# Attention on one core: the powers transposed 64 queries at a time, in two halves of the array

## The chip, the cores and the metric

The kernel runs on one core of a Trainium2 chip. A core has TensorE (PE in the profile; its weight loads are listed as PEld), VectorE (DVE), ScalarE (ACT), GpSimd (POOL) and SyncE (SP), each with its own queue of instructions, and 16 DMA engines. The metric is the device time of one execution in microseconds, lower is better; the median of the runs is compared.

## The reference, cut to what matters

One inference step of a two-layer network over 1024 prompt tokens and 32 sample tokens of width 1024: a recurrent layer (RG-LRU), then shared keys and values, then one layer of attention in a sliding window with 16 heads of 64 in 4 groups (g), and a sink per head. Keys come in chunks of 64: a query sees its own chunk and the two before it.

```python
s = jnp.einsum('bnqkgd,bnskd->bnkgqs', qb, kb).astype(jnp.float32) * scale
...
s = jnp.where(valid[None, :, None, None, None, :], s, -jnp.inf)
sink = sinks.astype(jnp.float32).reshape(N_KV_HEADS, GROUP)[None, None, :, :, None, None]
p = sink_softmax(s, sink)      # exp(s - m) / (sum exp(s - m) + exp(sink - m))
o = jnp.einsum('bnkgqs,bnskd->bnqkgd', p.astype(vb.dtype), vb)
```

Everything is float32. The kernel gets its accuracy from float32r matmuls by splitting each operand into a high and a low part.

## The kernel before, in words

Channels lie on partitions and tokens in columns, in three blocks of about 384 tokens. The recurrent layer and the projections of k and v come first; the attention begins at 549 us and ends at 826 us of the span; the output projection of the rest and the last norms follow.

The attention loops over the 4 groups g, and in each over nine stages j: j = 0 to 7 are 128 queries of the prompt each, for the group's 4 heads (nh = 4), j = 8 the 32 sample tokens, whose 4 heads share the 128 rows (nh = 1). A stage sees nk blocks of 128 keys: one for j = 0, two for the others. One stage has four steps:

- stage_s: S matmuls (L984), queries on the rows; VectorE takes the negated maximum (L986) and ScalarE the powers exp(s - m) with their sum (L989) into the tile P, 128 queries x nh heads x keys.
- stage_n: P is divided by the sum, two heads on ScalarE (L999), two on VectorE (L1001).
- stage_t: P has to be transposed, keys on partitions, for the next matmul. In a transpose on TensorE, P's 128 x 128 block is loaded as weights and the identity `ident` is passed through. The results of the nh heads for one block of keys go into one PSUM bank T (tag "T", two banks). `split` (L128, L129) moves each bank into ph (ScalarE, rounded to float32r) and pl (VectorE, the remainder).
- stage_o: O = V times ph and pl, summed over the blocks of keys in one bank (L1019). V holds a high and a low part in 64 columns each, so rows 64 to 127 of O are copied aside by ScalarE (L1021, `oh`) and added by VectorE (L1027) into the output tile TT, one head at a time.

Between the steps the loop in `_trunk` draws from a generator `fillers(g)`: matmuls of the gates (`gB`), of the next group's queries (`rAq`, `rBq`) or of the output projection (`obm`), all at L757. The order of each engine's queue isn't the order of this code: a scheduler that simulates the engines chooses it when the program is built. `pin` keeps an instruction in the order of the code in relation to others that are pinned. Each queue is then worked through strictly in the order that the scheduler left.

Of the kernel before, what the change touches and what calls it, by code (L numbers as in the profile page):

```python
# [10 lines left out]
F32R = mybir.dt.float32r  # L11
AF = mybir.ActivationFunctionType
ALU = mybir.AluOpType
# [4 lines left out]
P = 128  # L18
# [57 lines left out]
def _trunk(ctx, tc, nc, A):  # L76
    V, S, G = nc.vector, nc.scalar, nc.gpsimd
# [13 lines left out]
    def pin(i, on=True):  # L91
        return tc.keep_in_program_order(i) if on else i

    def bank(name, tag="mm", bufs=None):
        return psum.tile([P, 512], F32, tag=tag, name=name, bufs=bufs or nbank)
# [28 lines left out]
    def split(dst_hi, dst_lo, src, lo_eng=None, hi_dve=False, behind=False):  # L124
        if hi_dve:
            V.tensor_copy(dst_hi, src)
        else:
            pin(S.activation(dst_hi, src, AF.Copy), behind)  # L128
        (lo_eng or V).tensor_tensor(dst_lo, src, dst_hi.bitcast(F32), op=ALU.subtract)  # L129
# [131 lines left out]
    ident = cst.tile([P, P], F32, name="ident")  # L261
# [218 lines left out]
    half = {}  # L480
# [57 lines left out]
    def unit(name, dt=F32, w=384):  # L538
        return units.tile([P, 416], dt, tag="u", bufs=NU, name=name)[:, :w]
# [81 lines left out]
    for n in range(3):  # L621
        for m in LATE:
            w = NSB[n][1] - NSB[n][0]
            hl = [late.tile([P, 384], F32R, tag="t", bufs=NT, name=f"y{x}{m}_{n}")[:, :w] for x in "hl"]
# [86 lines left out]
    for n, order in enumerate(orders):  # L711
        zs, acc = {}, []
        w = NSB[n][1] - NSB[n][0]
# [25 lines left out]
    def att_tile(name, shape, dt, tag, bufs):  # L739
        return att.tile([P] + shape, dt, tag=tag, bufs=bufs, name=name)  # L740

    def kv_tile(name, shape, dt, tag, bufs=1):
        return kvp.tile([P] + shape, dt, tag=tag, bufs=bufs, name=name)
# [159 lines left out]
    QU, KU, VU, SG, TT = {}, {}, {}, {}, {}  # L903
# [56 lines left out]
    def stage_s(g, j):  # L960

        smp = j == 8
        n = 2 if smp else j // 3
        if (g, n) not in KU:
            load_kv(g, n)
        nm = f"{g}_{j}"
        nh, nk = (1 if smp else 4), (1 if j == 0 else 2)
        t0 = 3 if smp else max(j - 1, 0) - KB0[n] // P
        w = nk * P
        ks = slice(t0 * P, t0 * P + 256)  # L970
        sm = att_tile(f"sm{nm}", [3, 4], F32, "sm", 4)
        nmax, rsum, rl = (sm[:, i, :nh] for i in range(3))
        sk = slice(16 + g, 17 + g) if smp else slice(4 * g, 4 * g + 4)
        msk = smask if smp else mask[:, 256 - w:]

        pt = att_tile(f"P{nm}", [4, 258], F32, "P", 2)
        S.activation(pt[:, :nh, w:w + 1], nsnk[:, sk].unsqueeze(2), AF.Copy)
        for h0 in range(0, nh, 2):
            sb = bank(f"S{nm}_{h0}", "S", 2)
            for h in range(h0, min(h0 + 2, nh)):  # L980
                q = QS[g].rearrange("p h c -> p (h c)") if smp else QU[g, n][:, h, P * j - NSB[n][0]:P * j - NSB[n][0] + P]
                s = sb[:, (h - h0) * 256:(h - h0) * 256 + 256]
                for hl in range(2):
                    pin(nc.tensor.matmul(s, q, KU[g, n][:, hl, ks], start=hl == 0, stop=hl == 1), g == 0 and j == 0)  # L984
            for h in range(h0, min(h0 + 2, nh)):
                V.tensor_tensor_reduce(pt[:, h, :w], sb[:, (h - h0) * 256:(h - h0) * 256 + w], msk,  # L986
                                       -0.125, nsnk[:, sk][:, h:h + 1], op0=ALU.add, op1=ALU.min,
                                       accum_out=nmax[:, h:h + 1])
                S.activation(pt[:, h, :w + 1], pt[:, h, :w + 1], AF.Exp, bias=nmax[:, h:h + 1], scale=-1.0,  # L989
                             accum_out=rsum[:, h:h + 1])  # L990
        return dict(P=pt, nh=nh, nk=nk, t0=t0, n=n, nm=nm, smp=smp, w=w, rsum=rsum, rl=rl)
# [9 lines left out]
                V.tensor_scalar(pt[:, h, :w], pt[:, h, :w], rl[:, h:h + 1], None, op0=ALU.mult)  # L1001

    def stage_t(st):
        nm, w = st["nm"], st["nh"] * P
        st["p"] = []
        for kt in range(st["nk"]):
            tb = bank(f"T{nm}_{kt}", "T", 2)[:, :w]
            for h in range(st["nh"]):
                nc.tensor.transpose(tb[:, h * P:(h + 1) * P], st["P"][:, h, kt * P:(kt + 1) * P], ident)  # L1009
            hl = [att_tile(f"p{x}{nm}_{kt}", [512], F32R, "p" + x, 2)[:, :w] for x in "hl"]  # L1010
            split(*hl, tb)
            st["p"].append(hl)

    def stage_o(g, j, st):
        n, w, nk = st["n"], st["nh"] * P, st["nk"]
        ob = bank(f"O{st['nm']}", "O", 1)[:, :w]
        for kt in range(nk):
            for i, x in enumerate(st["p"][kt]):
                nc.tensor.matmul(ob, VU[g, n][:, st["t0"] + kt, :], x, start=kt + i == 0, stop=kt == nk - 1 and i == 1)  # L1019
        half = kv_tile(f"oh{st['nm']}", [512], F32, "oh")  # L1020
        S.activation(half[:64, :w], ob[64:128], AF.Copy)  # L1021
        q = w // 4
        c0 = 256 if st["smp"] else P * j - NSB[n][0]
        if (g, n) not in TT:
            TT[g, n] = [unit(f"T{g}_{n}_{i}", w=NSB[n][1] - NSB[n][0]) for i in range(2)]
        for h in range(4):
            V.tensor_tensor(TT[g, n][h // 2][64 * (h % 2):64 * (h % 2) + 64, c0:c0 + q],  # L1027
                            ob[:64, h * q:(h + 1) * q], half[:64, h * q:(h + 1) * q], op=ALU.add)

    ogl = {}  # L1030

# [87 lines left out]
    for g in range(4):  # L1119
        fil = fillers(g)  # L1120
        per = PER[g]
        todo = [0, 1, 2]
        st = {0: stage_s(g, 0)}
        stage_n(st[0], False)
        for j in range(9):
            if j < 8:
                st[j + 1] = stage_s(g, j + 1)
            if g == 0 and j == 0:
                for _ in range(2):
                    next(fil)  # L1130
            stage_t(st[j])
            if j < 8:
                stage_n(st[j + 1])
            for _ in range(per - (g == 3 and j > 6)):
                next(fil, None)
            stage_o(g, j, st.pop(j))
            while todo and j >= (2, 5, 8)[todo[0]] and (2 * g + 1, todo[0]) in SG:
                finish_og(g, todo.pop(0))
        if g == 3:
            break  # L1140
        run(fil)
        for n in todo:
            finish_og(g, n)
# [176 lines left out]
```

## Time and profile before

| | |
|---|---|
| median of 3 runs | 897.91 us (897.18 to 900.01) |
| the profiled execution | 896.39 us, of which its span is 894.6 us |
| TensorE busy | 881.0 us, 5462 matmul passes, mean clock granted 0.997 |
| weight loads busy | 863.1 us |
| VectorE, ScalarE, GpSimd busy | 702.3, 563.6, 211.5 us |

Busy shares are shares of the span. Matmuls overlap in the pipeline and their ends are modelled, so the durations of neighbouring matmuls add up to more than the time they take; the step from one start to the next tells what one costs. In rows of groups the columns are the shape (rows*columns of the array, then partitions x elements), the count after x, the busy time in us, the mean duration in ns, and the idle time of the engine ahead of them. Rows of the timeline begin with start and length in us and end with the number of instructions merged in them. Rows of a tile's table give the shortest, median and longest duration in ns, then first and last start in us. Rows of the table of stretches give the stretch and its length in us, busy time and count for PE, PEld, DVE, ACT and POOL, the granted clock, the DMA share and GB/s.

### The profile page before, as it was taken

Reading aid. Unit: us, or ns where it says so; the run is one execution under the profiler, and the core shown is the slowest. Engines: PE = TensorE matmul, PEld = TensorE weight load, DVE = VectorE, ACT = ScalarE, POOL = GpSimd, SP = SyncE. Lnnn points to the kernel's source line nnn. Section 1 sums busy time; section 2 is a strip of 40 time slices with the busy share of each in tenths; the row PEclk is TensorE's granted clock in tenths of the full one; section 3 lists DMA queues with packets and bytes.
Section 4 is the critical chain, followed back from the end, with each engine's and each line's share of the span. In section 5 each row is a group of like instructions: output and inputs, shape, how many; then the busy total and the mean of one; then the engine's idle time right before and its main releaser. Section 6 shows DMA issues by size and latency. Waiting matters only on the chain.

```text
span 894.6 us, 15865 instructions
## 1 busy us (share of the span) xinstructions
PE 881.0 (98%) x5462; PEld 863.1 (96%) x5462; DVE 702.3 (79%) x1511; ACT 563.6 (63%) x1233; POOL 211.5 (24%) x257
## 2 busy tenths in 40 slices
PE   9999999999999999999998999999999999999996
PEld 8999999999999999999997999999999999999996
DVE  5877878879897654176889847879999999898777
ACT  7848878789354325355675317756767767797652
POOL 5260212134300001124343532113023011002240
PEclk9999999999999999999999999999999999999999
DMA  9533433352544226446455568336448338444984
GB/s 335 199 107 108 118 100 120 110 147 86 182 128 126 91 55 209 136 133 202 145 171 175 190 183 231 97 101 192 115 125 228 99 120 233 118 135 123 300 259 170
DMA packets 96129, 138.76 MB, mean 155 GB/s; under 512 B 16224, under 2 KB 64128, under 8 KB 96048
## 3 DMA queue, kind: packets, MB, share of 16 engines
q1 hardware_dynamic: 86232, 124.24, 45.6%
q10 hardware_dynamic: 9640, 12.96, 4.8%
q8 instruction: 43, 0.70, 0.3%
q0 software_dynamic: 176, 0.54, 0.2%
q14 instruction: 38, 0.31, 0.1%
HBM read 99.54 MB, written 32.13 MB: 147 GB/s over the span
## 4 chain that ended last, share of the span: by engine, by line
PE 66%; DVE 4%; ACT 2%; DMA 2%; issue 1%; POOL 1%; SPq 0%; DVEq 0%; ACTq 0%; POOLq 0%
PE gB L757 10%; PE rAq L757 5%; PE rBq L757 5%; PE obm L757 5%; PE oa L168 5%; PE oa L167 5%; PE oa L169 5%; PE gb L167 4%; PE gb L168 4%; PE gb L169 4%; PE S L984 3%; PE O L1019 3%; PE T L1009 3%; PE ot L757 2%; PE rAk L757 1%
## 5 line engine op out<-in xcount | busy, mean ns | idle before, releaser
L167 PE MATMUL oa<-yh,whi_outa 128*128 128x384 f32 (+1 forms) x264 | 85.8, 326 | 0.0
L168 PE MATMUL gb<-xlo,whi_ina 128*128 128x384 f32 (+1 forms) x264 | 85.6, 324 | 0.0
L167 PE MATMUL gb<-xhi,whi_ina 128*128 128x384 f32 (+1 forms) x264 | 85.3, 323 | 0.1
L169 PE MATMUL gb<-xhi,wlo_ina 128*128 128x384 f32 (+1 forms) x264 | 85.4, 323 | 0.0
L169 PE MATMUL oa<-yh,wlo_outa 128*128 128x384 f32 (+1 forms) x264 | 85.2, 323 | 0.0
L168 PE MATMUL oa<-yl,whi_outa 128*128 128x384 f32 (+1 forms) x264 | 85.1, 323 | 0.0
L675 POOL TENSOR_TENSOR qp<-qp,qp 128x384 f32<-128x384 f32 (+2 forms) x34 | 42.2, 1242 | 178.5 <-ACT qp L673 166.4
L168 PE MATMUL br<-xlo,whi_ina 128*128 128x384 f32 (+1 forms) x240 | 77.7, 324 | 0.0
L167 PE MATMUL br<-xhi,whi_ina 128*128 128x384 f32 (+1 forms) x240 | 77.7, 324 | 0.0
L169 PE MATMUL br<-xhi,wlo_ina 128*128 128x384 f32 (+1 forms) x240 | 77.5, 323 | 0.0
L129 DVE TENSOR_TENSOR wlo_outa<-raw_outa,whi_outa 128x512 fp32r<-128x512 f32 (+1 forms) x60 | 43.0, 731 | 43.1 <-ACT whi_outa L128 42.9
L989 ACT ACTIVATE P<-P,sm 128x257 f32<-128x257 f32 (+1 forms) x132 | 64.3, 489 | 13.1 <-DVE sm L986 12.8
L757 PE MATMUL gB<-xl,whi_g 128*128 128x384 f32 (+1 forms) x192 | 63.1, 329 | 0.0
L757 PE MATMUL gB<-xh,whi_g 128*128 128x384 f32 (+1 forms) x192 | 63.1, 329 | 0.0
L128 ACT ACTIVATE whi_outa<-raw_outa 128x512 fp32r<-128x512 f32 (+1 forms) x60 | 35.5, 594 | 43.4 <-PE oa L168 23.9
L757 PE MATMUL gB<-xh,wlo_g 128*128 128x384 f32 (+1 forms) x192 | 62.8, 327 | 0.0
L986 DVE CUSTOM_DVE_ANT_0 P<-S,mask,nsnk 128x256 f32<-128x256 f32 (+1 forms) x128 | 53.1, 461 | 5.5 <-PE S L984 5.4
L257 DVE SCALAR_TENSOR_TENSOR conv<-ext,pa,conv 128x1060 f32<-128x1060 f32 (+2 forms) x51 | 46.1, 926 | 11.0 <-ACT conv L255 10.5
L167 PEld LDWEIGHTS gb<-xhi,whi_ina 128*128 128x128 f32 x264 | 49.7, 188 | 0.4 <-DVE u L565 0.4
L167 PEld LDWEIGHTS oa<-yh,whi_outa 128*128 128x128 f32 x264 | 49.6, 188 | 0.4
L168 PEld LDWEIGHTS oa<-yl,whi_outa 128*128 128x128 f32 x264 | 49.6, 188 | 0.4
L169 PEld LDWEIGHTS oa<-yh,wlo_outa 128*128 128x128 f32 x264 | 49.7, 188 | 0.0
(316 smaller groups left out, 2889.4 us busy)
## 6 DMA issues: line engine op xcount, KB each, us to landing
raw_ina<-w_in_a SPq DMA_DIRECT2D x44, 256.0 KB, 3.6
raw_outa<-w_out_a SPq DMA_DIRECT2D x40, 256.0 KB, 3.1
raw_ob<-w_out_b SPq DMA_DIRECT2D x32, 256.0 KB, 3.2
qscr<-quadq SPq DMA_DIRECT2D x8, 768.0 KB
Q<-qscr SPq DMA_DIRECT2D x32, 192.0 KB, 3.8
hscr<-u SPq DMA_DIRECT2D x11, 530.0 KB, 2.7
xr<-xr SPq DMA_DIRECT2D x8, 512.0 KB, 8.9
raw_g<-w_in_b SPq DMA_DIRECT2D x16, 256.0 KB, 5.2
```

Source lines behind the costliest of these rows:

```text
L128: pin(S.activation(dst_hi, src, AF.Copy), behind)
L129: (lo_eng or V).tensor_tensor(dst_lo, src, dst_hi.bitcast(F32), op=ALU.subtract)
L167: pin(nc.tensor.matmul(ps, wh, xh, start=i == 0, stop=False), behind and i == 0 or mid and i == n // 2)
L168: nc.tensor.matmul(ps, wh, xl, start=False, stop=False)
L169: nc.tensor.matmul(ps, wl, xh, start=False, stop=last and i == n - 1)
L257: V.scalar_tensor_tensor(c, e[:, c0 + k:c1 + k], pa[:, t, k:k + 1], c, op0=ALU.mult, op1=ALU.add)
L675: G.tensor_tensor(sums[0], sums[0], q, op=ALU.add)
L757: nc.tensor.matmul(ps, l, r, start=c == 0, stop=c == 3 * n - 1)
L984: pin(nc.tensor.matmul(s, q, KU[g, n][:, hl, ks], start=hl == 0, stop=hl == 1), g == 0 and j == 0)
L986: V.tensor_tensor_reduce(pt[:, h, :w], sb[:, (h - h0) * 256:(h - h0) * 256 + w], msk, -0.125, nsnk[:, sk][:, h:h + 1], op0=ALU.add, op1=AL ...
L989: S.activation(pt[:, h, :w + 1], pt[:, h, :w + 1], AF.Exp, bias=nmax[:, h:h + 1], scale=-1.0, accum_out=rsum[:, h:h + 1])
L1009: nc.tensor.transpose(tb[:, h * P:(h + 1) * P], st["P"][:, h, kt * P:(kt + 1) * P], ident)
```

## The change

A transpose now takes 64 queries instead of 128: half i of the queries lies on partitions 64 i to 64 i + 63, so its load uses that half of the array's rows (128 columns as before), with the matching 64 x 64 block of the identity passed through. Each half has a T bank of its own, for all heads and all blocks of keys, and the instructions alternate between the halves and are pinned. A bank is then split at once into half of ph and pl: these are now one tile each per stage, for both blocks of keys, with the columns of a block ordered by half of queries, then head, then query. stage_o's adds read that order; for j = 8 each half holds two heads and nothing is reordered.

```diff
     def stage_t(st):
-        nm, w = st["nm"], st["nh"] * P
-        st["p"] = []
-        for kt in range(st["nk"]):
-            tb = bank(f"T{nm}_{kt}", "T", 2)[:, :w]
-            for h in range(st["nh"]):
-                nc.tensor.transpose(tb[:, h * P:(h + 1) * P], st["P"][:, h, kt * P:(kt + 1) * P], ident)
-            hl = [att_tile(f"p{x}{nm}_{kt}", [512], F32R, "p" + x, 2)[:, :w] for x in "hl"]
-            split(*hl, tb)
-            st["p"].append(hl)
+        nm, nh, nk = st["nm"], st["nh"], st["nk"]
+
+        hl = [att_tile(f"p{x}{nm}", [2, 512], F32R, "p" + x, 1) for x in "hl"]
+        tb = [bank(f"T{nm}_{i}", "T", 2)[:, :nk * nh * 64] for i in range(2)]
+        for kt in range(nk):
+            for h in range(nh):
+                for i in range(2):
+                    r = slice(64 * i, 64 * i + 64)
+                    c = (kt * nh + h) * 64
+                    pin(nc.tensor.transpose(tb[i][:, c:c + 64], st["P"][r, h, kt * P:(kt + 1) * P], ident[r, r]))
+        for i in range(2):
+            split(*(x[:, :nk, i * nh * 64:(i + 1) * nh * 64] for x in hl),
+                  tb[i].rearrange("p (k c) -> p k c", k=nk))
+        st["p"] = [[x[:, kt, :nh * P] for x in hl] for kt in range(nk)]
...
         for h in range(4):
-            V.tensor_tensor(TT[g, n][h // 2][64 * (h % 2):64 * (h % 2) + 64, c0:c0 + q],
-                            ob[:64, h * q:(h + 1) * q], half[:64, h * q:(h + 1) * q], op=ALU.add)
+            dst = TT[g, n][h // 2][64 * (h % 2):64 * (h % 2) + 64, c0:c0 + q]
+            if smp:
+                a, b = (x[:64, h * q:(h + 1) * q] for x in (ob, half))
+            else:
+                a, b = (x[:64, :512].rearrange("p (i h c) -> p i h c", i=2, h=4)[:, :, h, :] for x in (ob, half))
+                dst = dst.rearrange("p (i c) -> p i c", i=2)
+            V.tensor_tensor(dst, a, b, op=ALU.add)
```

The program has 5675 matmuls instead of 5427 (248 transposes become 496), and four more splits on each of ScalarE and VectorE; no other count of working instructions differs. What the scheduler makes of it shows in TensorE's queue. In the rows, T_5_0 is stage j = 5 with the block of keys (before) or the half of queries (after) as the last index; further numbers are buffers. First, group g = 0 around the transposes of j = 5, before:

```order
L1019 MATMUL O_4_6799<-ph_4_1_6744,V_1_6468 128x512
L984 MATMUL S_6_2_6829<-K_2_6810,Q_2_6192 128x256 x2
L1019 MATMUL O_4_6799<-pl_4_1_6745,V_1_6468 128x512
L984 MATMUL S_6_2_6829<-K_2_6810,Q_2_6192 128x256 x2
L1009 MATMUL T_5_0_6838<-ident,P_5_6710 128x128 x4
L1009 MATMUL T_5_1_6847<-ident,P_5_6710 128x128 x4
L757 MATMUL rAq_1_6872<-xh_1_4834,whi_qA_0_6657 128x384
```

The same place in the changed program:

```order
L1013 MATMUL T_5_0_6871<-ident,P_5_6735 128x64
L757 MATMUL rAq_1_6909<-xl_1_4835,whi_qA_0_6682 128x384
L757 MATMUL rAq_1_6909<-xh_1_4834,wlo_qA_0_6683 128x384
L1024 MATMUL O_4_6830<-pl_4_6756,V_1_6481 128x512
L1024 MATMUL O_4_6830<-ph_4_6755,V_1_6481 128x512
L1024 MATMUL O_4_6830<-pl_4_6756,V_1_6481 128x512
L1013 MATMUL T_5_1_6872<-ident,P_5_6735 128x64
L1013 MATMUL T_5_0_6871<-ident,P_5_6735 128x64
L1013 MATMUL T_5_1_6872<-ident,P_5_6735 128x64
```

The first transpose of half 0 now stands alone, ahead of the end of the stage before; the other 15 follow behind it in one run (three of them are shown). This is so in 27 of the 36 stages, which makes 63 separate runs of transposes in all; before, there are 57.

Second, group g = 3 around the end of the transposes of j = 2, before:

```order
L1009 MATMUL T_2_0_9365<-ident,P_2_9218 128x128 x2
L1019 MATMUL O_1_9326<-pl_1_1_9253,V_0_9068 128x512
L1009 MATMUL T_2_0_9365<-ident,P_2_9218 128x128 x2
L1009 MATMUL T_2_1_9374<-ident,P_2_9218 128x128 x4
L757 MATMUL gB_1_9388<-xl_1_4911,whi_g_0_9152 128x384
L757 MATMUL gB_1_9388<-xh_1_4910,wlo_g_0_9153 128x384
```

And in the changed program, from the last two of the 15:

```order
L1013 MATMUL T_2_0_9527<-ident,P_2_9372 128x64
L1013 MATMUL T_2_1_9528<-ident,P_2_9372 128x64
L1024 MATMUL O_2_9615<-ph_2_9525,V_0_9215 128x512
L984 MATMUL S_5_0_9741<-K_1_9497,Q_1_9048 128x256 x4
L984 MATMUL S_5_2_9750<-K_1_9497,Q_1_9048 128x256 x4
L1013 MATMUL T_3_0_9651<-ident,P_3_9505 128x64
L1024 MATMUL O_2_9615<-pl_2_9526,V_0_9215 128x512
```

Before, the stage's first O matmul comes some 30 rows behind its transposes, with fillers between; now it stands right behind them. The same holds for g = 2, j = 7.

More of the change, by code (lines that the diff above doesn't have):

```diff
@@ L1022, in stage_o @@
         q = w // 4
+        smp = st["smp"]
         c0 = 256 if st["smp"] else P * j - NSB[n][0]
```

## The prediction

> **What bounds the kernel now.** I read the share of busy time by engine first, then the stretch of the attention alone, because the change touches nothing outside it.
>
> ```profile
> span 894.6 us, 15865 instructions
> PE 881.0 (98%) x5462; PEld 863.1 (96%) x5462; DVE 702.3 (79%) x1511; ACT 563.6 (63%) x1233; POOL 211.5 (24%) x257
> ...
> 549.00:826.00 277.00, 277.00 (x1806) 270.55 (x1805) 248.62 (x747) 203.18 (x571) 45.76 (x43) 1.00 0.49 142
> ```
>
> The last row is the table of stretches: from the first transpose (549 us) to the end of the attention (826 us) TensorE is busy for all 277.00 us, at full clock (1.00). VectorE (248.62) and ScalarE (203.18) have room beside it. A busy share alone can hide stalls, since the ends of matmuls are modelled, so I next looked for waits. The three longest of TensorE's in the whole run are these, and within 549 to 826 us the view of waits lists none.
>
> ```profile
> PE ss_x L188 <- POOL qx L675: 3.3, 1, 3.3
> PE warmup L110 <- DVE epst L107: 1.1, 1, 1.1
> PE vc L169 <- DVE wl_v L133: 0.5, 2, 0.3
> ```
>
> So in the attention TensorE is the bound: each microsecond that its queue gets longer or shorter is a microsecond of the run, and no other engine's work needs a price unless it makes TensorE wait.
>
> **What a transpose costs now.** The groups by line keep the transposes apart, and the timeline has one stage of them:
>
> ```profile
> L1009 PE MATMUL T<-ident,P 128*128 128x128 f32 x248 | 36.3, 272 | 0.0
> ...
> 644.04 1.04 PE L1009 MATMUL T<-ident,P 128*128 128x128 f32 x8
> 644.84 0.42 PE L757 MATMUL rAq<-xh,whi_qA 128*128 128x384 f32 x1
> 645.10 0.34 PE L757 MATMUL rAq<-xl,whi_qA 128*128 128x384 f32 x1
> ```
>
> Eight transposes take 1.04 us from the first start to the last end, and one alone lasts 0.272: the step from one to the next is (1.04 - 0.272) / 7 = 0.11 us, and I use 0.109. The 248 transposes thus hold the array for 248 x 0.109 = 27.0 us. That is all the change can win.
>
> What sets that step, the load of the weights (P, 128 columns) or the pass of the identity? The table of the tile's instructions and the only transposes with a narrower load tell:
>
> ```profile
> L1009 PEld LDWEIGHTS T<-ident,P x248: 136/141/146, 548.9 to 818.0; 128*128 128x128 f32 x124
> ...
> L839 PEld LDWEIGHTS v<-ident,vc x18: 94/139/145, 489.3 to 540.2; 128*128 128x128 f32 x16, 128*32 128x32 f32 x2
> ...
> 540.10 0.29 PE L757 MATMUL rBq<-xh,wlo_qB 128*128 128x288 f32 x1
> 540.23 0.38 PE L839 MATMUL v<-ident,vc 128*32 128x128 f32 x2
> 540.37 0.38 PE L757 MATMUL rBq<-xh,whi_qB 128*128 128x288 f32 x1
> 540.59 0.29 PE L757 MATMUL rBq<-xl,whi_qB 128*128 128x288 f32 x1
> ```
>
> At 540.23 us two transposes load only 32 columns (94 ns against 141) and still step by 0.38 - 0.27 = 0.11 us. So it is the pass of 128 columns of identity that takes 0.109 us, and 64 columns should take 0.055. The load's rate comes from the same two rows: 96 columns fewer are 47 ns less, so 128 columns are an estimated 0.062 us. That is for one full-height load; no run here shows a 64-row one.
>
> **The change, part by part.** *Transposes.* 248 of 128 columns become 496 of 64. If the two halves of the array work at the same time, a pair costs the longer of the two, the load's 0.062, that is 0.031 a piece. If they work one after the other a piece costs 0.055 (the pass alone) to 0.062. The far end, if a load alternating between halves hides behind nothing, is the full step of 0.109. No row shows two halves at work; I take 0.031, since operands, weights, and PSUM banks of a pair share nothing, and keep the others as rivals.
>
> *Entering and leaving the half-height mode.* Before, all transposes use the array at full height. Only one matmul of the kernel (two passes) is lower: the last of L329's, for the 32 sample tokens, with 32 rows. It is in the block at 46.88 us; the block at 27.54 has six passes of full height, so the two can be compared.
>
> ```profile
> L329 PEld LDWEIGHTS rs<-diag,ones x18: 182/191/193, 27.4 to 47.5; 128*128 128x128 f32 x16, 32*128 32x128 f32 x2
> ...
> 27.54 0.83 PE L329 MATMUL rs<-diag,ones 128*128 128x128 f32 x6
> 28.12 0.42 PE L167 MATMUL br<-xhi,whi_ina 128*128 128x384 f32 x1
> 28.38 0.33 PE L168 MATMUL br<-xlo,whi_ina 128*128 128x384 f32 x1
> ...
> 46.71 0.99 PEld L329 LDWEIGHTS rs<-diag,ones 128*128 128x128 f32 x6
> 47.74 0.19 PEld L167 LDWEIGHTS br<-xhi,whi_ina 128*128 128x128 f32 x1
> ...
> 46.88 0.94 PE L329 MATMUL rs<-diag,ones 128*128 128x128 f32 x6
> 47.75 0.45 PE L167 MATMUL br<-xhi,whi_ina 128*128 128x384 f32 x1
> 48.03 0.33 PE L168 MATMUL br<-xlo,whi_ina 128*128 128x384 f32 x1
> ```
>
> With six full-height passes the second br matmul starts 28.38 - 27.54 = 0.84 us after the block's start; with four full and two low ones, 48.03 - 46.88 = 1.15 us. One visit to the low mode costs 0.31 us, although its two passes are shorter. The loads say how: the load at 47.74 starts at the same time as its matmul (47.75) instead of ahead of it, so the array ran empty and the load lay open.
>
> The Trainium skill, in "TensorEngine Tiling (Array Packing)", section "Tiling Modes", Key Properties, says that changing the mode, not just the tile, drains TensorE. The 0.31 us agrees; the 32-column transposes at 540.23, a mode of their own by that page's list, show no such gap (0.14 us from 540.23 to 540.37, and 0.22 to the next, the usual hand-over). By the page's rule the sum is the one below; by the 32-column rows it is that of the rival without a drain.
>
> The order of the changed program has 63 separate runs of transposes in 36 stages: in 27 stages the first one stands alone, with other matmuls behind it, and the rest come later. Each run is a visit: 0.31 us, and 0.109 for its last transpose's hand-over to the next full load. The others follow at 0.031. Sum: 63 x 0.42 + 433 x 0.031 = 26.5 + 13.4 = 39.9 us, against 27.0: 12.9 us more. Half of the pass time is indeed won inside the blocks, and the visits cost more than that.
>
> *Splits.* Each half now has a bank, and both banks are full only after all 16 transposes, where before the first bank was ready after four. Both halves' split must be done before the first O matmul.
>
> ```profile
> L128 ACT ACTIVATE ph<-T x68: 254/594/602, 551.0 to 822.3; 128x512 fp32r<-128x512 f32 x60, 128x128 fp32r<-128x128 f32 x8
> L129 DVE TENSOR_TENSOR pl<-T,ph x68: 274/681/693, 551.6 to 823.5; 128x512 fp32r<-128x512 f32 x60, 128x128 fp32r<-128x128 f32 x8
> ```
>
> In two stages (g = 2, j = 7 and g = 3, j = 2) the new order puts the O matmul right behind the stage's transposes. There TensorE must wait for two ph of 0.594 us: 1.2 us each, 2.4 in all. The later end is one pl of 0.681 and a queued instruction of like length on each engine as well, about 2.5 us in each place and some more where the distance is about 1 us (g = 2, j = 4): 7 us. I take 3, near the lower end, since S matmuls stand behind the first O at one of them. Four stages (j = 0) split in two halves of 256 instead of once 512: four more on each of ScalarE and VectorE, covered by the 28 us that VectorE has idle in the stretch.
>
> *The rest.* stage_o issues as many adds (144) of as many elements, only strided; no DMA is added, and ones that the order moves on SP by a place or two feed weights that TensorE doesn't wait for today. The two split tiles of a kind become one of the same total size; the next stage's split then waits for all of O, which the order already puts ahead of it.
>
> Sum: 894.6 + 12.9 + 3 = 910.5 us of span. The profiled execution took 896.39, 1.8 more than its span, and the median is 1.5 above that, so 913.8: I forecast 914, 1.8% slower.
>
> **Rivals.**
> - *The halves take turns* (0.055 to 0.062 a piece). 26.5 + 433 x 0.055 = 50.3, or 53.3: 23 to 26 us more, with the waits 926. For it: the eight transposes above step evenly, one pass behind the other, and nothing in the trace runs two at a time. Against it: all of those use the same rows of the array. The Trainium skill, "TensorE: Matmul & The Clock Gate", Part 3, states that matmuls in different row groups run concurrently and start about 4 ns apart; by that rule this rival falls, and no run here shows it.
> - *No drain between full height and half.* For it: the 32-column transposes slip in without a gap. Then 63 x 0.109 + 433 x 0.031 = 20.3 us, 6.7 less than now; with 3 of waits 3.7 us are won: 894. This ends on the other side. It decides where a visit costs under (27.0 - 3 - 20.3) / 63 = 0.06 us, against 0.31 measured.
> - *No drain, but turns.* 6.9 + 433 x 0.058 = 32.0: 5 more, 3 of waits: 906.
> - *A half-height load costs the full step, in turn.* For it: the shortest load of L329's, 32-row ones among them, is 182 ns against a median of 191, so fewer rows hardly shorten a load. Against it: those aren't transposes, whose load is shorter (141). 26.5 + 433 x 0.109 = 73.7, which is 46.7 more, with the waits 948.
>
> **How the numbers follow.** A measurement here tells about 0.3% (2.7 us) from no change. Forecast 0.46 (its own range 909 to 920: a visit 0.05 us cheaper, the difference of the loads' 0.109 and 0.062, or as much dearer, and waits of 2.4 to 7), turns 0.29, no drain 0.11, no drain with turns 0.07, full loads 0.05, the rest 0.02. The first two and the 906 case hold 0.82: 904 to 930. Faster: the no-drain case, part of which lands within 0.3%: 0.09, same 0.04, slower 0.87.
>
> **What would show it.** The 496 transposes should step by about 0.03 us inside a block (0.055 or more: turns); the first matmul behind a block should start with its own load, about 0.2 us late, 63 times (no gap: no drain); TensorE should wait at O in two or three places for ph. VectorE's busy time should stay near 702 us. Wrong would be a stage of 16 that takes less than 0.55 us with its neighbours undisturbed: then the visits are free.

## The result, and the profile after

The changed kernel takes 923.77 us (median of 4, 922.0 to 924.46) against 897.54: the ratio is 1.0285, 95% interval 1.0259 to 1.0311. It is slower, and inside the range, but 10 us above the point of the forecast and above the 909 to 920 that the forecast's own case allowed. The profiled execution took 924.17 us. Its page and, from the groups and the tile's table, its transposes:

```profile
span 922.4 us, 16386 instructions
PE 897.9 (97%) x5710; PEld 861.1 (93%) x5710; DVE 703.1 (76%) x1515; ACT 566.1 (61%) x1237; POOL 210.8 (23%) x257
...
L1013 PE MATMUL T<-ident,P 64*128 64x64 f32 x496 | 30.8, 235 | 0.0
...
L1013 PEld LDWEIGHTS T<-ident,P x496: 134/138/224, 550.1 to 846.3; 64*128 64x128 f32 x166
L1013 PE MATMUL T<-ident,P x496: 221/223/366, 550.1 to 846.4; 64*128 64x64 f32 x166
```

The work of the other engines is the same (VectorE 703.1 us, 702.3 before); TensorE is busy longer and has a smaller share of the span. The timeline of one undisturbed stage (g = 0, j = 1) shows a visit to the half-height mode:

```profile
555.68 0.33 PE L757 MATMUL gB<-xh,whi_g 128*128 128x384 f32 x1
555.86 0.34 PE L757 MATMUL gB<-xl,whi_g 128*128 128x384 f32 x1
556.12 0.71 PE L1013 MATMUL T<-ident,P 64*128 64x64 f32 x16
556.76 0.45 PE L757 MATMUL gB<-xh,wlo_g 128*128 128x384 f32 x1
557.04 0.34 PE L757 MATMUL gB<-xh,whi_g 128*128 128x384 f32 x1
557.22 0.34 PE L757 MATMUL gB<-xl,whi_g 128*128 128x384 f32 x1
```

Sixteen transposes take 0.71 us to the end of the last, which is 0.22 long: (0.71 - 0.22) / 15 = 0.033 us a step, where the forecast had 0.031. Start by start the trace shows it more sharply: the second half's transpose follows 0.003 to 0.004 us behind the first half's, the next pair 0.057 to 0.059 later. So the halves do run at the same time. What the visit costs is spread over four steps: in, the step from 555.86 to 556.12 is 0.26 instead of 0.18; the first pair takes 0.05 longer than the others; the last transpose to the next matmul is 0.15, some 0.09 more than from pair to pair; and out, 0.28 from 556.76 to 557.04 instead of 0.18. The stage's eight full transposes took 0.87 us before; here, from 0.08 ahead of the block to 0.10 behind it, it is 0.64 + 0.18 = 0.82. Such a stage wins 0.05 us, so even 32 of them would win under 2 us.

In 27 stages the first transpose stands alone. One of them (g = 0, j = 6):

```profile
597.11 0.40 PE L984 MATMUL S<-K,Q 128*128 128x256 f32 x2
597.44 0.27 PE L1013 MATMUL T<-ident,P 64*128 64x64 f32 x1
597.64 0.44 PE L757 MATMUL rBq<-xh,whi_qB 128*128 128x384 f32 x1
597.92 0.39 PE L1024 MATMUL O<-pl,V 128*128 128x512 f32 x1
...
598.71 0.71 PE L1013 MATMUL T<-ident,P 64*128 64x64 f32 x15
599.35 0.44 PE L757 MATMUL rBq<-xl,whi_qB 128*128 128x384 f32 x1
```

One transpose takes 0.20 us to the next start and makes the matmul behind it another 0.10 late: two visits for one stage.

That is the smaller part of the loss. The view of waits for TensorE between 549 and 847 us, empty before, now reads:

```profile
PE O L1024 <- DVE T L1039: 3.0, 2, 1.6
PE gB L757 <- DVE su L952: 2.3, 2, 1.4
PE S L984 <- DVE sm L986: 1.7, 3, 1.0
PE rBq L757 <- DVE rp2q L774: 0.7, 1, 0.7
PE gB L757 <- DVE rp2q L774: 0.7, 1, 0.7
PE O L1024 <- DVE pl L129: 0.2, 1, 0.2
```

That is 8.6 us, in five stages: g = 2, j = 1, 4 and 7, and g = 3, j = 1 and 2. (The T of L1039 is not the bank: it is stage_o's output tile TT.) The timeline of three of them, the last with the ScalarE and VectorE work that O waits for, and the table of stretches (the figure ahead of the DMA share is the mean granted clock):

```profile
705.83 0.70 PE L1013 MATMUL T<-ident,P 64*128 64x64 f32 x15
707.96 0.40 PE L757 MATMUL gB<-xh,whi_g 128*128 128x288 f32 x1 [1.43 <-DVE su L952]
...
784.92 0.71 PE L1013 MATMUL T<-ident,P 64*128 64x64 f32 x15
786.62 0.74 PE L984 MATMUL S<-K,Q 128*128 128x256 f32 x4 [0.99 <-DVE sm L986]
788.28 0.40 PE L757 MATMUL gB<-xh,whi_g 128*128 128x288 f32 x1 [0.92 <-DVE su L952]
...
794.99 0.70 PE L1013 MATMUL T<-ident,P 64*128 64x64 f32 x15
795.96 1.08 ACT L128 ACTIVATE ph<-T 128x512 fp32r<-128x512 f32 x2
796.01 1.17 DVE L1039 TENSOR_TENSOR T<-O,oh 64x128 f32<-64x128 f32 x4
797.33 0.47 PE L1024 MATMUL O<-ph,V 128*128 128x512 f32 x1 [1.64 <-DVE T L1039]
798.17 1.56 PE L984 MATMUL S<-K,Q 128*128 128x256 f32 x8 [0.37 <-DVE sm L986]
...
800.77 0.63 PE L1024 MATMUL O<-ph,V 128*128 128x512 f32 x1
801.20 0.63 PE L1024 MATMUL O<-pl,V 128*128 128x512 f32 x1
...
762.03:765.44 3.41, 1.50 (x7) 1.22 (x8) 3.34 (x12) 1.59 (x5) 1.32 (x2) 1.00 1.03 294
765.44:768.86 3.42, 3.42 (x13) 3.42 (x12) 3.38 (x15) 2.32 (x11) 0.25 (x1) 0.50 0.11 42
785.93:789.34 3.41, 1.80 (x12) 1.60 (x13) 3.32 (x14) 3.38 (x12) 0.00 (x0) 1.00 0.04 15
789.34:792.75 3.41, 3.41 (x16) 3.31 (x15) 3.09 (x8) 2.00 (x6) 0.00 (x0) 0.50 0.00 0
796.17:799.58 3.41, 1.80 (x9) 1.25 (x9) 3.33 (x14) 3.41 (x12) 0.00 (x0) 1.00 0.43 137
799.58:806.41 6.83, 6.68 (x36) 5.55 (x35) 6.70 (x23) 5.57 (x16) 0.00 (x0) 0.50 0.33 108
```

At g = 3, j = 2 O stands right behind its 15 transposes and waits 1.64 us: the two ph end at 797.04, the adds of the stage before, which empty O's only bank, at 797.18. The same happens at g = 2, j = 7 (1.35 us). At g = 2, j = 1 and g = 3, j = 1 no O, but gB and S stand behind the 15, and wait for banks that VectorE empties late. Behind three of the five stages the clock that TensorE is granted falls to half, for 3.4, 3.4 and 6.8 us. A matmul of 512 columns steps there by 0.43 us (800.77 to 801.20) instead of 0.232, so of these 13.7 us about 6 are lost.

Since matmuls overlap, I made the account from the steps between starts, from the first transpose to the last. Other matmuls get the step that they have undisturbed, by width (0.232 us for 512 columns, 0.175 for 384, 0.133 for 288, 0.119 for 256); what is over inside and next to a run of transposes is theirs, and what is over elsewhere, or above 0.3 us there, is waiting or half clock. Where a run is followed by a long wait, a slightly different cap moves 2 or 3 us between the transposes and the waits of the table, so these two are no sharper than that.

| us | before | after | change | forecast |
|---|---|---|---|---|
| stretch | 269.6 | 297.0 | +27.4 | +15.9 |
| transposes | 27.4 | 38.8 | +11.4 | +12.9 |
| waits and half clock | 0.2 | 16.4 | +16.3 | +3 |
| other matmuls | 242.1 | 241.6 | -0.5 | 0 |

The waits of the view and the half clock make 8.6 + 6 of the 16.3; the rest is not put down to anything.

### The profile page after: what moved, and what is told of

It reads as the page before. It is cut to its first block, busy times and chain, and to the rows that moved or that the text cites. A ratio compares the mean times of both kernels' runs of the same rounds, so it can differ in the third digit from the quotient of the medians.

```text
span 922.4 us, 16386 instructions
## 1 busy us (share of the span) xinstructions
PE 897.9 (97%) x5710; PEld 861.1 (93%) x5710; DVE 703.1 (76%) x1515; ACT 566.1 (61%) x1237; POOL 210.8 (23%) x257
## 4 chain that ended last, share of the span: by engine, by line
PE 68%; DVE 5%; ACT 2%; DMA 1%; issue 1%; POOL 0%; DVEq 0%; ACTq 0%
PE gB L757 11%; PE obm L757 8%; PE rBq L757 5%; PE rAq L757 5%; PE oa L169 4%; PE oa L168 4%; PE oa L167 4%; PE gb L167 3%; PE gb L168 3%; PE gb L169 3%; PE S L984 3%; PE O L1024 3%; PE T L1013 3%; PE ot L757 2%; PE rBk L757 1%
## 5 line engine op out<-in xcount | busy, mean ns | idle before, releaser
L757 PE MATMUL gB<-xh,whi_g 128*128 128x384 f32 (+1 forms) x192 | 65.3, 340 | 3.0 <-DVE su L952 2.3
L1039 DVE TENSOR_TENSOR T<-O,oh 64x128 f32<-64x128 f32 (+1 forms) x144 | 39.2, 272 | 28.7 <-ACT oh L1026 26.7
```

The costliest lines, as they stand in the source:

```text
L757: nc.tensor.matmul(ps, l, r, start=c == 0, stop=c == 3 * n - 1)
L1039: V.tensor_tensor(dst, a, b, op=ALU.add)
```

## The experiments

The theory to be tested had three terms: a visit to the half-height mode has a price; inside it the halves overlap; and the waits come from the order that the pinned transposes get, not from the mode. The account by the same rules for each (waits with the half clock):

| kernel | median us | ratio (95%) | runs of transposes | transposes | waits |
|---|---|---|---|---|---|
| free_halves | 909.5 | 1.0130 (1.0110 to 1.0151) | 59 | 39.3 | 1.6 |
| full_pinned | 915.8 | 1.0200 (1.0161 to 1.0239) | 57 | 29.3 | 16.4 |
| full_free | 900.5 | 1.0037 (1.0025 to 1.0048) | 64 | 28.1 | 4.1 |
| halves_apart | 918.1 | 1.0221 (1.0201 to 1.0242) | 72 | 49.5 | 0.2 |
| one_visit | 957.5 | 1.0682 (1.0655 to 1.0709) | 36 | 29.0 | 53.8 |
| before_pinned | 898.4 | 1.0009 (0.9999 to 1.0019) | 70 | 27.6 | 1.9 |
| halves_twice | 916.9 | 1.0210 (1.0184 to 1.0235) | 46 | 48.5 | 0.2 |
| full_twice | 924.2 | 1.0293 (1.0267 to 1.0319) | 53 | 54.5 | 0.1 |

**free_halves: without the pins**

```diff
-                    pin(nc.tensor.transpose(tb[i][:, c:c + 64], st["P"][r, h, kt * P:(kt + 1) * P], ident[r, r]))
+                    nc.tensor.transpose(tb[i][:, c:c + 64], st["P"][r, h, kt * P:(kt + 1) * P], ident[r, r])
```

> The changed kernel without the pins on the transposes: the same 496 half-height transposes, but the scheduler may float them. Its order has 59 runs of transposes (63 with the pins), 354 steps between the halves and 83 within one half, and no O matmul closer than 3.2 us of matmul work behind its stage's transposes. Theory (three terms: visits to the half-height mode, halves that overlap, and waits that the pinned order makes): 59 x 0.42 + 354 x 0.031 + 83 x 0.062 = 40.9 us against 27.4 in the kernel before, 13.5 more, and the 16 us of waits and of half clock gone: 911 us. Rival (the waits and the half clock come from the half-height mode itself, not from the order): again 924 or more.

Measured 909.5, as the theory had it. The view of waits for 549 to 833 us has one row left, and no half clock:

```profile
PE O L1024 <- DVE pl L129: 0.4, 1, 0.4
```

So the mode alone costs 12 us, and the waits belong to the order.

**full_pinned and full_free: full height in the new flow**

```diff
+        half = max(nh // 2, 1)
+        tb = [bank(f"T{nm}_{i}", "T", 2)[:, :nk * half * P if nh > 1 else P] for i in range(2)]
         for kt in range(nk):
-            for h in range(nh):
-                for i in range(2):
...
+            for h in (0, 2, 1, 3) if nh > 1 else (0,):
+                i, c = (h // 2, (kt * 2 + h % 2) * P) if nh > 1 else (kt, 0)
+                pin(nc.tensor.transpose(tb[i][:, c:c + P], st["P"][:, h, kt * P:(kt + 1) * P], ident))
...
```

full_free is the same without pin. stage_o's adds read the columns by head, as before.

> Full-height transposes of 128 queries as in the kernel before, but in the changed kernel's flow: two heads to a bank, both banks full only after the last transpose, one ph and one pl tile a stage, and pinned. Its order has O directly behind the transposes in three places. Theory: no visits, transposes 27 us as before, and waits of the same kind as in the changed kernel, 10 to 16 us with the half clock that follows them: 907 to 914 us. Rival (the waits come from the mode): 898.

> The same as full_pinned without the pins; no O matmul close behind its transposes. Both theories: 898 us, within 3, since neither a visit nor a pinned order is left; if the new flow itself (split of both banks ahead of the first O) costs something, it shows here.

full_pinned has no low transpose, and 16.4 us of waits, as many as the changed kernel. Its timeline and stretches show the same picture:

```profile
786.66 0.93 PE L1012 MATMUL T<-ident,P 128*128 128x128 f32 x7
789.03 0.50 PE L1025 MATMUL O<-ph,V 128*128 128x512 f32 x1 [1.44 <-ACT ph L128]
...
684.00:687.00 3.00, 2.68 (x10) 2.68 (x11) 3.00 (x13) 2.13 (x8) 1.56 (x2) 0.64 0.21 44
790.00:793.00 3.00, 2.46 (x11) 2.02 (x10) 3.00 (x10) 2.11 (x9) 0.00 (x0) 0.61 0.13 48
```

Its 915.8 lies 2 us above the expectation's end, and its runs spread from 912 to 919. Without pins it is 900.5: 3 us are left to the flow itself, at the upper edge of what was expected, and 4.1 of waits are there in the account (of its slowest run, 903.2). The rival, that the mode makes the waits, is out.

**before_pinned: pins alone**

```diff
-                nc.tensor.transpose(tb[:, h * P:(h + 1) * P], st["P"][:, h, kt * P:(kt + 1) * P], ident)
+                pin(nc.tensor.transpose(tb[:, h * P:(h + 1) * P], st["P"][:, h, kt * P:(kt + 1) * P], ident))
```

> The kernel before with nothing changed but pins on its 248 transposes. 70 runs of transposes, none with an O close behind. Theory (pins harm only together with the new flow, where both banks must be full before the first O): 898 us, within 3. Rival (the pins alone make the waits): 907 to 914.

898.4: no difference. The pins alone make no waits, the new flow alone some 3 us; the two together make 16. What the pins keep is the order of the transposes among themselves: the S matmuls are pinned only at g = 0, j = 0, and O never. That the scheduler has less to choose from when two banks both wait for the last of 16 transposes in a kept order is argued, not shown. halves_apart, next, fits it: it is pinned and in the new flow, but its first bank is full after eight, and it has 0.2 us of waits. Why O, S or gB come to stand right behind the transposes in just these places I did not follow up.

**halves_apart: one half after the other**

```diff
-        for kt in range(nk):
-            for h in range(nh):
-                for i in range(2):
+        for i in range(2):
+            for kt in range(nk):
+                for h in range(nh):
```

> The changed kernel with the loop over the halves outermost: all transposes of half 0, then all of half 1, still pinned. 72 runs, 393 steps within one half and 31 between. Theory (alternating halves overlap, one half alone steps at its load's 0.062): 72 x 0.42 + 393 x 0.062 + 31 x 0.031 = 55.6 us, 28 more than before, 926 us, with no O close behind its transposes. Rival (the step of 0.031 has nothing to do with the halves, a half-height transpose is simply that short): 72 x 0.42 + 424 x 0.031 = 43.4, 16 more, 914.

918, between the two, and by the time alone nearer to the rival's 914. The steps decide. A run of 16 in its timeline:

```profile
564.75 1.01 PE L1013 MATMUL T<-ident,P 64*128 64x64 f32 x16
565.69 0.44 PE L757 MATMUL gB<-xh,whi_g 128*128 128x384 f32 x1
565.97 0.34 PE L757 MATMUL gB<-xl,whi_g 128*128 128x384 f32 x1
```

It takes (1.01 - 0.22) / 15 = 0.053 a step instead of 0.033. Start by start, behind the first one the early and the late steps are 0.061 to 0.063, as the load's estimate had it: within one half a step is twice the 0.031, so the rival is out. But around the change of halves in the middle some come in pairs (0.006 or 0.007, then 0.054 to 0.056). The semaphore that the last transpose of the first half raises comes with the 11th start, not the 8th, so by this trace three of the second half started among the first half's last. So the overlap is shown, and because it sets in here too, the loss was sized too high: 49.5 us of transposes instead of 55.6.

**one_visit: both banks as one tile**

```diff
-        tb = [bank(f"T{nm}_{i}", "T", 2)[:, :nk * nh * 64] for i in range(2)]
+        tb2 = psum.tile([P, 2, 512], F32, tag="T", name=f"T{nm}", bufs=1)
+        tb = [tb2[:, i, :nk * nh * 64] for i in range(2)]
...
```

The part left out gives the transposes at the very end (L1199) other banks.

> The changed kernel with the two T banks as one tile of two banks, so that a stage's first transpose waits for both to be free (the transposes at the very end, L1199, use other banks). Its order has 36 runs of transposes, one a stage, all alternating between the halves, and six places where O follows within 0.5 to 2.6 us of matmul work. Theory: 36 x 0.42 + 460 x 0.031 = 29.4 us of transposes against 27.4 before: one visit a stage only breaks even, 2 us more; with 2 to 5 us of waits at the short places 902 us (900 to 905), so not below the kernel before even so. Rival (a visit costs little and 27 lone transposes cost something else): the transposes fall to about 20 us, and the time to 893 to 897.

The transposes came out as expected (29.0 us, expected 29.4), the time did not: 957.5, a miss by 55 us. The next stage's transposes can't start before both banks are split, and TensorE waits for what VectorE and ScalarE do late, at half clock for long:

```profile
665.52 0.72 PE L1014 MATMUL T<-ident,P 64*128 64x64 f32 x16
668.42 2.03 PE L984 MATMUL S<-K,Q 128*128 128x256 f32 x8 [2.18 <-DVE sm L986]
...
638.50:641.50 3.00, 3.00 (x14) 3.00 (x14) 3.00 (x10) 3.00 (x10) 0.00 (x0) 0.50 0.00 0
669.30:675.50 6.20, 6.02 (x19) 5.73 (x20) 5.01 (x12) 3.16 (x9) 1.98 (x2) 0.50 0.00 1
696.60:706.50 9.90, 7.85 (x36) 6.92 (x37) 7.21 (x25) 5.20 (x17) 3.59 (x4) 0.50 0.24 83
```

Its two numbers with those of the changed kernel give the price list: 63 a + 433 s = 38.8 and 36 a + 460 s = 29.0 make a visit with its first transpose a = 0.395 us and each further step s = 0.032. Both kernels have long waits, which blur this. Single runs with nothing waiting beside them say the same: from the start of the matmul ahead of a run to the second start behind it, less the two plain steps, the median is 0.40 us for a lone transpose (changed kernel), 0.84 for 16 (free_halves) and 1.34 for 32 (halves_twice, below), so 0.031 a step; eight at full height take 0.88 (kernel before).

**halves_twice and full_twice: more transposes in a visit**

```diff
-        for kt in range(nk):
+        for kt in [*range(nk)] * 2:
```

This is free_halves; full_twice is the kernel before with `for h in [*range(st["nh"])] * 2`.

> free_halves with every stage's transposes done twice into the same places (the second writes what the first wrote). Its order has 46 runs, 904 steps between the halves, 42 within one. Theory: 46 x 0.42 + 904 x 0.031 + 42 x 0.062 = 50.0 us of transposes, 22.6 more than the kernel before: 920.5 us, and 0 to 3 of waits; 4 us below full_twice, because a visit now carries up to 32. Rival (a half-height transpose is no cheaper, the visits' price in the other runs was really the transposes'): 79 us of transposes, twice those of free_halves, 949.

> The kernel before with every stage's transposes done twice into the same places: 496 of 0.109 = 54.1 us, 27 more: 925 us. Rival for the 0.109 (part of it is only the hand-over to the next matmul, so that the second round costs less): below 920.

One visit of halves_twice, and one stage of full_twice, from their timelines:

```profile
600.33 1.21 PE L1013 MATMUL T<-ident,P 64*128 64x64 f32 x32
```

```profile
601.81 1.91 PE L1009 MATMUL T<-ident,P 128*128 128x128 f32 x16
```

(1.21 - 0.22) / 31 = 0.032 and (1.91 - 0.27) / 15 = 0.109: both prices hold. 916.9 is 3.6 us below its expectation and 7.2 below full_twice (924.2, expected 925). With 32 transposes to a visit, the halves win.

## Why the prediction was right, and where it was not

- *The time, 914 in a range of 904 to 930*: the direction and the transposes' part came out as argued, but that 923.8 lies in the range is in part luck. The sum's own case ended at 920; the range reached further only for the rival of turns, which is wrong.
- *TensorE is the bound*: held. free_halves lost 12.3 us with 11.9 more of transposes.
- *A full transpose 0.109, set by the pass of the identity*: held: full_twice repeats the 0.109, and in halves_apart 64 columns of identity step by 0.062 within one half although their load has as many columns, so those don't set the 0.109. *Halves at the same time, 0.031*: 0.033 in the row, 0.032 by the price list. The rival of turns would have put the time at 926, close to what came out, and it is wrong all the same; its transposes would have taken 50 us. By the time alone it would have passed for right.
- *A visit 0.31, with the hand-over 0.42*: measured 0.395, where the prediction had only a single matmul of 32 rows to read it from. The sign that it gave, a load lying open for about 0.2 us behind a block, is not how it looks: the cost is spread over the steps in and out. *63 visits*: all there. The term was 12.9 and measured 11.4. The rule from the Trainium skill, "TensorEngine Tiling (Array Packing)", Key Properties, that a change of mode drains, agrees with it here too.
- *Waits of 3 us, at most 7*: this step failed, with 16.3 measured. The term looked for places where O stands behind its own transposes and priced two ph splits there, 1.2 us each. At the two places that it named O waited 1.35 and 1.64 us: nearly that size, though VectorE's adds into TT, not ph, ended last, 0.1 us behind ph. What the term left out: the next matmuls behind these O, which waited for VectorE in their turn (0.7 and 0.4 us); g = 2, j = 1 and g = 3, j = 1, 3.3 us of waits, where gB and S and not O stand behind the transposes; and the half clock, 6 us, which it put at nothing. The third place that it named, g = 2, j = 4, has 1.0 us.
- *No drain, faster*: out; a lone transpose takes 0.40 us (median), not 0.109.

The best that the idea could have given is also clear. With a = 0.395, s = 0.032 and 0.109 for a full one, n low transposes in a visit break even where 0.395 + (n - 1) x 0.032 = n / 2 x 0.109, at n = 16: just one stage's number. The single runs put it a little lower: 0.84 us for 16 against 0.88 for eight at full height. One visit a stage with no wait would thus win some 1 us of 898, too little to tell from no change. Two stages in one visit would need four T banks; the kernel's eight PSUM banks are in use, and it wasn't tried. No run beat the kernel before.

## What to carry to other kernels

Price a change of the array's height by the visit, not by the matmul: about 0.36 us over the plain step here, so it pays from about 16 small transposes in one piece, and a scheduler that lets one of them slip ahead pays twice. Where one engine is never idle, look in the new order for consumers that stand right behind their producers: each is a wait, the queue behind it waits on, and several close together halve TensorE's clock, which here cost 6 us on top of 8.6. Look for every such consumer, not only for the one that the change touches: here gB and S stood there too. And compare the parts of the sum, not only the time: here a wrong rival would have given the right microseconds.

## What the runs showed of the hardware

The halves of the array overlap almost fully for transposes: in the stage shown the second starts 0.003 to 0.004 us behind the first, about what the Trainium skill, "TensorE: Matmul & The Clock Gate", Part 3, states for row groups (4 ns). Not expected was how little standing halves the clock: behind waits of 1.64 and 0.37 us with 15 transposes ahead of them, and of 1.44 us in full_pinned, where no single wait came near 3 us. The same page, Part 1, speaks of an idle window of about 3.4 us; here no wait was that long, and the measurement decides.

The traces show more of it. In each run every half-clock spell of the attention lasts 3.41 us or a multiple, and the spells begin whole multiples of 3.41 us apart (765.44, 789.34 and 799.58 in the changed kernel). In the stretch of 3.41 us just ahead of its three spells TensorE was busy for 1.50, 1.80 and 1.80 us, so it stood for over 1.6. Cut on this raster, the attention and what follows it has, over all ten traces, 14 stretches at full clock in which TensorE stood for over 1.6 us; 13 are followed by half clock, and no stretch in which it stood for less is. This is read off afterwards and not tested, but it fits the wait of 1.43 us at g = 2, j = 1, which no half clock follows: the raster cuts it into 0.88 and 0.54. So what seems to count is the sum of the waits within such a stretch, and not the longest. What the 0.395 us of a visit is made of, drain or open loads, was not separated.
